# Where the low parts of the weight tiles are subtracted in a decoder trunk with product-key experts

## Chip, cores, metric

The kernel runs on one core of one Trainium2 chip. The metric is device time in microseconds (us) of one execution; less is better. The engines are called PE (TensorE), DVE (VectorE), ACT (ScalarE), POOL (GpSimd) and SP (SyncE, which only issues DMAs here).

## What is computed

Two layers over 512 tokens of width 1024: a gated linear recurrence, then latent attention. Each is followed by a PEER layer, an expert layer whose 16384 experts are single neurons that are found by product keys. The change lies in the PEER layer alone, which runs once per layer:

```python
def peer(h, w_q, sub_keys, u_tab, v_tab):
    q = (h @ w_q).reshape(B, S, 8, 2, 128)                      # 8 heads, two halves
    s = jnp.einsum('bshpd,hpnd->bshpn', q, sub_keys)            # scores against 2 x 128 keys
    v1, i1 = lax.top_k(s[..., 0, :], 16)
    v2, i2 = lax.top_k(s[..., 1, :], 16)
    cand = (v1[..., :, None] + v2[..., None, :]).reshape(B, S, 8, 256)
    cv, ci = lax.top_k(cand, 16)
    idx = e1 * 128 + e2        # e1, e2: the keys of the 16 best pairs
    g = softmax(cv)
    act = gelu(h . u_tab[idx])
    out = sum(g * act * v_tab[idx])
```

## The kernel before

**Experts without a gather.** For the first 384 of the 512 tokens (`ND`) the kernel does not gather expert rows. It computes all 16384 expert activations as dense products, 128 tiles of 128 experts (`u_part`, tensor uT), multiplies them with a gate matrix that is zero where an expert was not chosen, and multiplies the result with all 128 tiles of v. For the last 128 tokens (`gather_steps`) POOL gathers rows of u and v by indirect DMAs, 256 per layer through four row buffers (`grow`, `GROWS`), and DVE takes the dot products and the weighted sums.

**hi and lo.** float32 products are made of three passes over pairs: each operand is split into a high part, rounded by ACT (`whi`), and a low part, the difference (`wlo`). `mm3` runs lo x hi, hi x lo and hi x hi. `wtile` loads a weight tile of 128x1024 (512 KB, SP's queue, four buffers `raw`), and `split` writes the two parts into three buffers each:

```python
last = nc.scalar.activation(hi, src, AF.Copy)
lo = (eng or nc.vector).tensor_tensor(lo, src, hi.bitcast(F32), op=OP.subtract)
```

The engine of the subtraction is an argument. In the profile it is line L165, whichever engine runs it; the rounding is L164, the matmuls are L201 to L203.

**The stages of `peer`.**

1. *Scoring.* Four groups of two heads. Each group has four tiles of w_pq (three of the first group's are made ahead of it), 16 key score matmuls (`sc`), then on DVE for each block of 128 tokens the search of the 16 best (`topk_half`: maxima, their indices, their replacement, twice) and the sums of pairs (`candidates`). Behind each group come a few modulation columns (`adas`, L153, on DVE; six per group in layer 0, two in layer 1) and `UPQ[grp]` expert tiles. The last group's search for the gathered token block is decoded there too (`decode`, one-hot products `oh`), which gives POOL its indices.
2. `UDEC` = 13 more expert tiles, while DVE decodes the first block of 128 tokens.
3. *Gate stretch.* 24 groups of 16 tokens (`gate_group`): DVE makes one-hot tiles `oo` and products `pr`, PE multiplies them into the gate matrix (`wps`), ACT copies it out and writes 1 MB per group to DRAM. Between groups the loop spreads the expert tiles that are left up to `LEAD - UEND` = 86, and 74 of the gather steps (`EARLY`). An expert tile planned for group i stands on PE behind the matmuls of group i-2. From tile 27 on an expert tile's activations go to DRAM (`gsp`, 192 KB, ACT's queue).
4. Seven more expert tiles, then the products with v, with the remaining expert tiles in between.

**What sets the order.** The program is traced in the order of the source; a planner then orders each engine's queue by a timeline of its own, by priority and readiness. `issue_after` adds an order between two instructions of one engine. The numbers in `UPQ`, `UDEC` and `UEND` are written by hand.

Of the kernel before, what the change touches and what calls it, by code (L numbers as in the profile page):

```python
# [23 lines left out]
KC = D // P  # L24
# [18 lines left out]
SPILL = 66  # L43
OWN = KC * T // ND
LEAD = OWN + RING - 3 + SPILL
UPQ = (5, 6, 6, 6)
UDEC = 13
UEND = 7
QUIET = 4
# [34 lines left out]
class Trunk:  # L84
# [953 lines left out]
    def peer(self, l):  # L1038
        nc, io, tc = self.nc, self.io, self.tc
        nd = NB - 1  # L1040
        with ExitStack() as st:
# [6 lines left out]
            h = []  # L1048
# [12 lines left out]
            with own:  # L1061
                for i, hs in enumerate(HALVES):
                    for k in range(KC):
# [5 lines left out]
                        hi, lo = (p[:, hs] for p in h[k])  # L1069
# [33 lines left out]
            def ring(t):  # L1103
                held = (t - OWN) % RING < RING - 3
                return acts.tile([P, ND], F32, name="gact" if held else "gsp", bufs=RING - 3 if held else 3)

            nc.scalar.dma_start(self.xscr, self.x)

            def u_part(after=None):
                t = state["u"]  # L1110
                state["u"] = t + 1
                out = self.bank("u", True)
                hi, lo = self.wtile(io["uT"][l][t], KC, eng=nc.vector)
                with tc.issue_after(after) if after is not None else ExitStack():
                    for k, (bh, bl) in enumerate(h):
                        self.mm3(out[:, :ND], (hi[:, k, :], lo[:, k, :]), (bh[:, :ND], bl[:, :ND]), k == 0, k == KC - 1)
                if t < OWN:
                    gact[t] = self.x.rearrange("p k t -> p (k t)")[:, t * ND:t * ND + ND]
                elif LEAD - SPILL <= t < LEAD:
                    g = acts.tile([P, ND], F32, name="gsp", bufs=3)  # L1120
                    nc.scalar.activation(g, out[:, :ND], AF.Gelu)
                    nc.scalar.dma_start(self.gscr[l, t - (LEAD - SPILL)], g)
                    return
                else:
                    gact[t] = ring(t)
                nc.scalar.activation(gact[t], out[:, :ND], AF.Gelu)  # L1126
# [13 lines left out]
            def decodes(bs):  # L1140
                for b in bs:
                    res = []
                    for _ in self.decode(dpool, cvs[b], cis[b], iu[b], res):
                        yield
                    if b == nd:
                        gsel.append(self.gather_index(gpool, l, *res))
                    else:
                        prep[b] = self.gate_prep(pool, *res)

            with tc.tile_pool(name=f"pq{l}", bufs=1) as pool:  # L1150
                for grp in range(4):
                    keys = pool.tile([P, 4, P], F32, name="keys", bufs=2)
                    nc.scalar.dma_start(keys, io["keysT"][l][:, 4 * grp:4 * grp + 4, :])
                    outs = []
                    wq = l * 16 + 4 * grp
                    if grp == 0:
                        outs = pq0
                    qs = []
                    for m in range(4):
                        if m >= len(outs):  # L1160
                            outs.append(self.bank("pq"))
                            self.lin(outs[m], self.wtile(io["w_pq"][wq + m], KC, eng=nc.vector), h)
                        q = pool.tile([P, T], F32, name="pq_s", bufs=5)
                        nc.scalar.activation(q, outs[m], AF.Copy)
                        qs.append(q)
                    for b in (nd, *range(nd)):
                        sc = self.bank("sc")
                        for m in range(4):
                            nc.tensor.matmul(sc[:, m * P:m * P + P], qs[m][:, b * P:b * P + P], keys[:, m, :],
                                             start=True, stop=True)  # L1170
                        for m in range(4):
                            last = self.topk_half(pool, sc[:, m * P:m * P + P], vs[b][:, 4 * grp + m, :],
                                                  iu[b][:, 4 * grp + m, :])
                        self.candidates(pool, vs[b], cvs[b], cis[b], 2 * grp, 2)
                        if grp == 3 and b == nd:
                            for _ in decodes((nd,)):
                                pass
                            gsteps = self.gather_steps(gpool, l, *gsel[0], hn)
                    self.hold = ()
                    with tc.issue_after(last):  # L1180
                        self.adas(6 if l == 0 else 2, pool)
                    for _ in range(UPQ[grp]):
                        u_part()
            with tc.tile_pool(name=f"gate{l}", bufs=1) as pool:
                nsg = P // TG
                steps = decodes(range(nd))
                for i in range(UDEC):
                    u_part()
                while 0 not in prep:
                    next(steps)  # L1190
                n0, nt = state["u"], nd * nsg
                ds = 0
                wlast, plast = [None, None], []
                for i in range(nt):
                    more = 1 if i >= nsg and i % nsg < nsg // 2 else 0
                    while state["u"] < n0 + (LEAD - UEND - n0) * (i + 1) // nt + more:
                        u_part(after=wlast[-2])
                    w, p = self.gate_group(pool, l, i // nsg, i % nsg, *prep[i // nsg])
                    wlast.append(w)
                    plast.append(p)  # L1200
                    while ds < 7 * (i + 2) // nsg:
                        next(steps, None)
                        ds += 1
                    with tc.issue_after(plast[max(0, i - 1)]):
                        while done < min(EARLY, EARLY * (i + 1) // (nt - QUIET)):
                            next(gsteps)
                            done += 1
                while state["u"] < LEAD:
                    u_part(after=wlast[-1])
# [113 lines left out]
            outs = [hpool.tile([P, D], F32, name=f"onat{b}", tag=f"h{b}") for b in range(nd)] + [next(gsteps)]  # L1323
# [232 lines left out]
```

## Time and profile before

| | |
|---|---|
| runs shown | 2972.43, 2970.81, 2964.76 us (median 2970.81) |
| the profiled execution | 2963.21 us, span 2961.4 us |
| granted PE clock, mean | 0.990 |
| busy: PE, DVE, ACT, POOL | 2874.9, 2559.4, 1387.6, 960.9 us |
| scoring to first gate product, layer 0 and 1 | 221 to 468 us, 1744 to 1980 us |
| gate groups, layer 0 and 1 | 468 to 728 us, 1980 to 2245 us |
| DMA over the span | 274 GB/s |

How to read it: times count from the span's start. A row of a group of instructions gives line, engine, operation, output <- input, shape, count, then busy us and mean ns, then idle us before them and what ended it. A row of a window gives, for each engine, busy us and in brackets the instructions. Matmuls are pipelined, so a mean length of a matmul is more than its share of PE's time.

### The profile page before, as it was taken

The page shows a single profiled execution, that of the slowest core. Times are in us where ns is not written, and L with a number is a line of the kernel's source. Part 1 is how long each engine was busy: PE and PEld are TensorE (multiplying, and loading weights), DVE is VectorE, ACT ScalarE, POOL GpSimd, SP SyncE. Part 2 cuts the span into 40 slices and gives each one's busy share as a digit, 9 for nine tenths or more (in the row PEclk, how much of TensorE's full clock was granted, in tenths as well). Part 3 has the DMA queues.
Part 4 walks back from the last instruction along what each step waited for, and adds up shares of the span by engine and source line. Part 5 has one row for each costly group of instructions (what it writes and reads, how often), then busy time and mean ns, then how long its engine had stood idle before and what let it go on. Part 6 is the DMA issues. An engine that isn't in the chain of part 4 may idle for free.

```text
span 2961.4 us, 43899 instructions
## 1 busy us (share of the span) xinstructions
PE 2874.9 (97%) x15680; PEld 2566.0 (87%) x15680; DVE 2559.4 (86%) x4887; ACT 1387.6 (47%) x2039; POOL 960.9 (32%) x718
## 2 busy tenths in 40 slices
PE   7999999989999999999999999999999999999998
PEld 5689898989888889998778799999989888899997
DVE  8989999999888878889878888999997777888888
ACT  4753245656343333333576742456655333333333
POOL 4000003645142234535434400015643111244542
PEclk9999999999999999999999999999999999999999
DMA  8544558999999999999323334369999999999996
GB/s 317 188 139 147 173 178 305 357 371 367 307 393 359 365 321 354 319 350 324 121 83 114 120 132 136 125 216 353 362 355 370 319 335 322 310 328 354 345 333 224
DMA packets 296219, 813.71 MB, mean 275 GB/s; under 512 B 33152, under 2 KB 130560, under 8 KB 289600
## 3 DMA queue, kind: packets, MB, share of 16 engines
q1 hardware_dynamic: 188928, 439.41, 43.4%
q0 software_dynamic: 78912, 287.34, 26.9%
q10 hardware_dynamic: 28160, 84.14, 7.3%
q8 instruction: 124, 2.03, 0.3%
q14 instruction: 95, 0.78, 0.1%
HBM read 727.44 MB, written 83.36 MB: 274 GB/s over the span
## 4 chain that ended last, share of the span: by engine, by line
PE 72%; DVE 15%; issue 5%; DMA 4%; POOL 2%; ACT 2%; ACTq 0%; DVEq 0%; SPq 0%; POOLq 0%
PE acc L202 11%; PE acc L203 11%; PE acc L201 11%; PE u L201 8%; PE u L202 8%; PE u L203 8%; DVE wlo L165 3%; POOL grow L1451 2%; DVE oo L1022 1%; DMA grow<-in_u_dram,idx 1%; DVE pr L1024 1%; PE pq L202 1%; PE pq L203 1%; DMA ada_raw<-in_adaw_dram 1%; PE pq L201 1%
## 5 line engine op out<-in xcount | busy, mean ns | idle before, releaser
L1451 POOL DMA_INDIRECT grow<-in_u_dram,idx x256 | 374.8, 1464 | 1099.2 <-DVE gdot L1455 404.4
L201 PE MATMUL u<-h,wlo 128*128 128x384 f32 x2048 | 692.8, 338 | 2.0 <-DVE wlo L165 1.0
L203 PE MATMUL u<-h,whi 128*128 128x384 f32 x2048 | 688.5, 336 | 0.0
L202 PE MATMUL u<-h,whi 128*128 128x384 f32 x2048 | 687.6, 336 | 0.0
L203 PE MATMUL acc<-vh,ah 128*128 128x512 f32 x1512 | 589.4, 390 | 0.0
L202 PE MATMUL acc<-vl,ah 128*128 128x512 f32 x1512 | 589.1, 390 | 0.0
L1451 POOL DMA_INDIRECT grow<-in_v_dram,idx x256 | 411.6, 1608 | 514.5 <-DVE gacc L1460 336.5
L201 PE MATMUL acc<-vh,al 128*128 128x512 f32 x1512 | 555.8, 389 | 0.0
L165 DVE TENSOR_TENSOR wlo<-raw,whi 128x1024 fp32r<-128x1024 f32 (+1 forms) x313 | 383.3, 1226 | 85.0 <-ACT whi L164 84.9
L165 DVE TENSOR_TENSOR vl<-vraw,vh 128x1024 fp32r<-128x1024 f32 x252 | 308.4, 1224 | 125.8 <-ACT vh L164 120.5
L164 ACT ACTIVATE whi<-raw 128x1024 fp32r<-128x1024 f32 (+2 forms) x362 | 352.4, 975 | 114.9 <-issue 33.2
L201 PEld LDWEIGHTS u<-h,wlo 128*128 128x128 f32 x2048 | 386.6, 189 | 6.1 <-ACT gact L1126 1.7
L202 PEld LDWEIGHTS u<-h,whi 128*128 128x128 f32 x2048 | 386.3, 189 | 2.7
L203 PEld LDWEIGHTS u<-h,whi 128*128 128x128 f32 x2048 | 385.8, 188 | 0.1
L203 PEld LDWEIGHTS acc<-vh,ah 128*128 128x128 f32 x1512 | 283.8, 188 | 59.2
L202 PEld LDWEIGHTS acc<-vl,ah 128*128 128x128 f32 x1512 | 283.8, 188 | 57.4
L201 PEld LDWEIGHTS acc<-vh,al 128*128 128x128 f32 x1512 | 283.8, 188 | 57.0
L1460 DVE SCALAR_TENSOR_TENSOR gacc<-grow,gdot,gacc 128x1024 f32<-128x1024 f32 x254 | 325.2, 1280 | 8.9 <-DMA grow<-in_v_dram,idx 7.8
L1455 DVE CUSTOM_DVE_ANT_0 grow<-grow,hn 128x1024 f32<-128x1024 f32 x256 | 309.7, 1220 | 20.9 <-DMA grow<-in_u_dram,idx 20.6
L164 ACT ACTIVATE vh<-vraw 128x1024 fp32r<-128x1024 f32 x252 | 264.6, 1050 | 97.0 <-issue 73.5
L164 ACT ACTIVATE ah<-gact 128x384 fp32r<-128x384 f32 x204 | 106.6, 523 | 390.0 <-PE acc L203 248.5
L1033 ACT ACTIVATE stg<-wps 128x512 f32<-128x512 f32 x192 | 185.0, 1120 | 40.4 <-PE wps L193 40.4
(417 smaller groups left out, 4342.9 us busy)
## 6 DMA issues: line engine op xcount, KB each, us to landing
raw<-in_uT_dram SPq DMA_DIRECT2D x256, 512.0 KB
vraw<-in_v_dram SPq DMA_DIRECT2D x256, 512.0 KB
wscr<-stg ACTq DMA_DIRECT2D x48, 1024.0 KB
wt<-wscr SPq DMA_DIRECT2D x42, 1024.0 KB
ada_raw<-in_adaw_dram SPq DMA_DIRECT2D x76, 512.0 KB
gscr<-gsp ACTq DMA_DIRECT2D x132, 192.0 KB
gact<-gscr SPq DMA_DIRECT2D x108, 192.0 KB
ada_raw<-in_adaw_dram POOLq DMA_DIRECT2D x36, 512.0 KB
```

The source lines that it names most:

```text
L164: last = nc.scalar.activation(hi, src, AF.Copy)
L165: lo = (eng or nc.vector).tensor_tensor(lo, src, hi.bitcast(F32), op=OP.subtract)
L201: nc.tensor.matmul(out, al, bh, start=first, stop=False, **kw)
L202: nc.tensor.matmul(out, ah, bl, start=False, stop=False, **kw)
L203: last = nc.tensor.matmul(out, ah, bh, start=False, stop=last, **kw)
L1022: nc.vector.tensor_tensor(oo.rearrange(by_pair, d=2), io, toks(et), op=OP.is_equal)
L1024: prod = nc.vector.tensor_tensor(pr.rearrange(by_pair, d=2), hot, toks(gp), op=OP.mult)
L1033: nc.scalar.activation(stg[:, :, c:c + 4].rearrange("p e t -> p t e"), wps.rearrange("p (t e) -> p t e", t=4), AF.Copy, scale=1.0 / GSCALE)
L1451: nc.gpsimd.indirect_dma_start(out=row, out_offset=None, in_=tabs[s], in_offset=bass.IndirectOffsetOnAxis(ap=idx[:, k:k + 1], axis=0))
L1455: nc.vector.tensor_tensor_reduce(row, row, hn, op0=OP.mult, op1=OP.add, scale=1.0, scalar=0.0, accum_out=col)
L1460: nc.vector.scalar_tensor_tensor(acc, row, col, acc, op0=OP.mult, op1=OP.add)
```

## The change

The subtractions of the weight tiles of w_pq (all but the three that are made ahead of the first group), of the expert tiles in the scoring and of the 13 `UDEC` tiles are issued on POOL in place of DVE. `UPQ` goes from 23 to 14 tiles per layer; since the gate loop takes what is left up to tile 86, nine more tiles come to stand there, and their subtractions stay on DVE.

```diff
-UPQ = (5, 6, 6, 6)
+UPQ = (3, 3, 4, 4)
...
-            def u_part(after=None):
+            def u_part(after=None, eng=None):
...
-                hi, lo = self.wtile(io["uT"][l][t], KC, eng=nc.vector)
+                hi, lo = self.wtile(io["uT"][l][t], KC, eng=eng or nc.vector)
...
-                            self.lin(outs[m], self.wtile(io["w_pq"][wq + m], KC, eng=nc.vector), h)
+                            self.lin(outs[m], self.wtile(io["w_pq"][wq + m], KC, eng=nc.gpsimd), h)
...
                     for _ in range(UPQ[grp]):
-                        u_part()
+                        u_part(eng=nc.gpsimd)
...
                 for i in range(UDEC):
-                    u_part()
+                    u_part(eng=nc.gpsimd)
```

## Prediction

> **What bounds the kernel now.** I read the page first: its busy line and the shares of the chain that ended last.
>
> ```profile
> PE 2874.9 (97%) x15680; PEld 2566.0 (87%) x15680; DVE 2559.4 (86%) x4887; ACT 1387.6 (47%) x2039; POOL 960.9 (32%) x718
> PE 72%; DVE 15%; issue 5%; DMA 4%; POOL 2%; ACT 2%; ACTq 0%; DVEq 0%; SPq 0%; POOLq 0%
> ```
>
> TensorE (PE) is all but full, VectorE (DVE) comes next, GpSimd (POOL) idles for two thirds. So time can only come from PE's gaps, and I looked for them in the stretches that the change touches: first key scores to first gate product, and the gate groups, in both layers (windows, columns as the header says).
>
> ```profile
> core 0: us, PE busy (x) PEld busy (x) DVE busy (x) ACT busy (x) POOL busy (x), PEclk, DMA share, GB/s
> 221.00:468.00 247.00, 244.17 (x1352) 230.96 (x1352) 236.41 (x1003) 96.13 (x128) 5.40 (x4) 1.00 0.54 176
> 468.00:728.00 260.00, 242.44 (x1846) 235.73 (x1845) 254.59 (x301) 161.65 (x199) 146.80 (x69) 0.98 0.97 355
> 1744.00:1980.00 236.00, 236.00 (x1315) 224.57 (x1314) 215.10 (x970) 94.43 (x124) 5.29 (x4) 1.00 0.44 143
> 1980.00:2245.00 265.00, 249.73 (x1884) 243.92 (x1883) 254.98 (x300) 163.43 (x203) 147.75 (x69) 0.97 0.96 352
> ```
>
> While keys are scored PE is full (244 of 247 us, 236 of 236); POOL does almost nothing. In the gate stretch PE lacks 17.6 and 15.3 us, DVE is 98% and 96% busy, and DMA is at 0.97. The waits (us in total, times, longest) say for whom PE waits:
>
> ```profile
> PE wps L1030 <- DVE pr L1024: 34.2, 19, 5.6
> ```
>
> That is the gate's one-hot products: the gate stretch is bound by DVE. With PE's granted clock at 0.98 and 0.97 there (260 x 0.02 + 265 x 0.03 = 13 us), all that this change can reach is 3 + 17.6 + 15.3 + 13 = about 49 us in both layers.
>
> **The change part by part.** Per layer, `UPQ` falls from 23 to 14 tiles. Of the subtractions in `wtile`, 13 for w_pq, 14 for uT in the scoring and 13 for uT in `UDEC` go to POOL: 40. The 9 moved tiles stay on DVE, inside the gate loop.
>
> ```profile
> L165 DVE TENSOR_TENSOR wlo<-raw,whi 128x1024 fp32r<-128x1024 f32 x50 | 60.7, 1214 | 0.0
> L165 POOL TENSOR_TENSOR wlo<-raw,whi 128x1024 fp32r<-128x1024 f32 x3 | 7.2, 2386 | 22.6 <-ACT whi L164 22.6
> 1925.00:1950.00 25.00, 25.00 (x146) 25.00 (x145) 24.86 (x93) 11.87 (x16) 0.00 (x0) 1.00 0.49 151
> ```
>
> One subtraction is 1.21 us on DVE and 2.39 us on POOL. In 1925 to 1950 PE runs u matmuls alone: 25 / 146 = 0.171 us each, 24 to a tile, 4.11 us a tile. POOL's 2.39 us is under that, and three hi/lo buffers stand between, so I cost POOL's length itself at nothing; if PE ran out of prepared tiles it would cost up to 2.4 - 1.2 = 1.2 us for each.
>
> *Before the gate.* PE gets 9 x 4.11 = 37 us less work there. DVE gets about 50 subtractions less (the row above): -61 us. What DVE may lose again is the question. No row shows POOL subtracting beside the key search, but the attention stage has POOL subtractions beside DVE work (timeline: start, length, engine, line, operation):
>
> ```profile
> 1444.78 4.86 POOL L165 TENSOR_TENSOR xlo<-raw,xhi 128x1024 fp32r<-128x1024 f32 x2 [2.98 <-ACT xhi L164]
> 1446.04 0.69 DVE L340 TENSOR_TENSOR xn<-x,rs 128x512 f32<-128x512 f32 x1 [1.21 <-PE rs L325]
> 1447.93 2.25 DVE L359 TENSOR_TENSOR hml<-hf,hmh 128x512 fp32r<-128x512 f32 x1
> 1450.70 0.68 DVE L165 TENSOR_TENSOR hml<-hf,hmh 128x512 fp32r<-128x512 f32 x1
> 1467.50 2.40 POOL L165 TENSOR_TENSOR wlo<-raw,whi 128x1024 fp32r<-128x1024 f32 x1 [17.87 <-ACT whi L164]
> 1467.87 2.45 DVE L165 TENSOR_TENSOR wlo<-raw,whi 128x384 fp32r<-128x384 f32 x1 [0.37 <-ACT whi L164]
> L165 DVE TENSOR_TENSOR al<-gact,ah 128x384 fp32r<-128x384 f32 x98 | 54.5, 557 | 16.3 <-ACT ah L164 16.3
> ```
>
> The same DVE operation on hml takes 0.68 us alone and 2.25 us beside POOL, ending 0.5 us after it; a 128x384 subtraction takes 2.45 instead of 0.56, again to POOL's end. Both read two SBUF tensors. xn at 1446.04, whose rs lies in PSUM, keeps its 0.69 us in the middle of a POOL subtraction. So a two-input SBUF operation of DVE stands still until POOL has finished. The Trainium skill, SBUF — State Buffer, section "SBUF: two separate sides", says the same: one port pair, an exclusive lock for the whole instruction, against a DVE instruction with two SBUF inputs or in a 2-port mode; the trace agrees with 2.25 against 0.68 us. By "a POOL subtraction is off the path" alone the change would gain as in the first rival; by the lock it is what follows.
>
> In 221 to 468 the search itself (maximum, index, replace) has one data tensor or its scores in PSUM, so I let it pass. These have two:
>
> ```profile
> L153 DVE CUSTOM_DVE_ANT_0 ada_junk<-ada_raw,csil,vecs 128x1024 bf16<-128x1024 f32 x24 | 30.8, 1282 | 9.0 <-DMA ada_raw<-in_adaw_dram 9.0
> L929 DVE TENSOR_TENSOR cand<-v 128x128 f32<-128x128 f32 x16 | 4.4, 274 | 0.0
> L932 DVE TENSOR_TENSOR cand<-v 128x96 f32<-128x96 f32 x16 | 3.9, 241 | 0.0
> L978 DVE TENSOR_TENSOR oh<-iota_m,rc 128x1024 bf16<-128x1024 bf16 x9 | 6.2, 692 | 0.2
> 221.03 0.52 DVE L918 MAX8 v<-sc 128x8 f32<-128x128 f32 x2 [0.74 <-PE sc L1169]
> 417.25 0.29 DVE L922 FIND_INDEX8 iu<-v,s 128x8 uint32<-128x128 f32 x1
> ```
>
> The last two rows are the first and the last of the search: 196 us, less up to 37. Scoring: 27 POOL subtractions are 64 us of some 165, so an isolated two-input operation meets one with chance 0.39 and waits half of 2.39. Layer 0 has 24 ada and 16 cand pairs: 40 x 0.39 x 1.2 = 19 us; layer 1 has 8 ada: 24 x 0.39 x 1.2 = 11 us. Decode: nine rounds of oh, each with a chain of two-input operations behind it, run while the 13 `UDEC` tiles are made; nearly each of the 13 POOL subtractions meets one soon after its start, 1.5 us each, 20 us. Estimate: DVE loses 39 us in layer 0 and 31 in layer 1. Bounds: nothing, and 40 x 2.39 = 96 us, if each meets one at its start. The rows above, 1.6 and 1.9 us lost, are nearer to the upper end for one meeting; the thin traffic of two-input operations in the search pulls down the average (0.9 us per subtraction). The upper bound would put layer 0 at -61 + 96 + 17 = +52; I leave it outside the range, since it asks that each of 40 be met in its first moment. The lock holds POOL as well; its 2.39 us leave 1.7 us of each tile's 4.11 for that.
>
> When does the first gate product start?
>
> ```profile
> 468.32 2.36 DVE L1024 TENSOR_TENSOR pr<-oo,gp 128x2048 f16<-128x2048 f16 x2
> 1979.96 2.35 DVE L1024 TENSOR_TENSOR pr<-oo,gp 128x2048 f16<-128x2048 f16 x2
> L165 DVE TENSOR_TENSOR wlo<-raw,whi 128x1024 fp32r<-128x1024 f32 x19 | 23.2, 1223 | 0.9 <-ACT whi L164 0.9
> ```
>
> Layer 0: DVE was busy 236 of 247 us, so DVE sets it: -61 + 39 = -22 us. Layer 1: DVE had 21 us idle, PE paces the scores. Seven of the nine tiles lay ahead of the last key group (2 + 3 + 2): -29 us; from its search (1890.6) to 1974 DVE made the 19 subtractions of the third row, -23 us, and meets the 20 us of lock of the decode: -3. Together -32; the 11 us of the scoring lie in DVE's idle time. PE's own bound is -37 in both.
>
> *The gate stretch.* It takes on 9 tiles, 8.8 of them by the last product: DVE +8.8 x 1.22 = 11 us, to 254.6 + 11 = 265; PE +8.8 x 4.11 = 36. PE's present need is its tiles and gate matmuls at undisturbed pace: 46 u tiles (1104 matmuls by the row below) x 4.11 = 189, and 742 others at 0.056 (469.60, 469.65, 469.71) = 42, together 231.
>
> ```profile
> 468.00:728.00 260.00, 200.62 (x1104) 0.98 0.97 355
> 469.60 0.22 PE L1030 MATMUL wps<-pr,oo 128*128 128x128 f16 x1 [2.14 <-DVE pr L1024]
> 469.65 0.22 PE L193 MATMUL wps<-pr,oo 128*128 128x128 f16 x1
> 469.71 0.22 PE L1030 MATMUL wps<-pr,oo 128*128 128x128 f16 x1
> ```
>
> So PE needs 267 and DVE 265, against 260 now. Two engines at the same load wait for each other in turn; I add 10 us (now 17 of gaps with 29 us of slack on PE): 277, +17 us per layer. The floor of this term is +7. What moves along: 9 loads of 512 KB on SP's queue and 9 spills of 192 KB on ACT's, 6.3 MB. 260 us x 355 GB/s = 92.3 MB; 98.6 MB in 277 us is 356 GB/s, the rate of now, so I add nothing; were DMA the bound there, the 6.3 MB would cost 18 us, just the term taken. ACT gets 9 x (1.0 + 0.5) = 13 us on 162 of 260: hidden.
>
> Sum: layer 0 -22 + 17 = -5, layer 1 -32 + 17 = -15: **-20 us**. The profiled execution took 2963.2 us (span 2961.4), so 2943; the three runs shown have a median of 2970.8, 7.6 us above. I put forecast and rivals on the middle, 2967: 2947.
>
> *POOL's queue.* The subtractions enter it ahead of the gathers:
>
> ```profile
> 446.88 1.62 POOL L1451 DMA_INDIRECT grow<-in_u_dram,idx  x1 [0.30 <-issue]
> 472.30 1.68 POOL L1451 DMA_INDIRECT grow<-in_u_dram,idx  x1 [23.79 <-DVE gdot L1455]
> ```
>
> The fifth gather waits 23.8 us for a row buffer. A subtraction queued behind it would wait as long, and PE behind that. In program order all 40 come first; the planner may reorder. Gathers that wait for a subtraction lose 2.4 us of that 23.8: nothing.
>
> **The rivals.**
>
> *The lock hardly bites* (DVE loses under 15 us per layer). For it: most of the search has one input. Then PE sets the start: -37 + 17 = -20 each, -40: 2927.
>
> *No change.* In the decode each of the 13 POOL subtractions holds DVE for its whole length, 31 us instead of 20: layer 0 -5 + 11 = +6, layer 1 -15 + 11 = -4, together +2: 2969. For it: DVE hardly idles there, and POOL would subtract 2.39 of each 4.11 us.
>
> *The search is held too* (the other side). Replace, index and maximum of the second eight read their scores from SBUF; if they count as the two-input ones do, a subtraction in the scoring costs DVE half its length nearly always, 1.2 us, beside the 31 us of the decode: 27 x 1.2 + 31 = 63 us. Layer 0: -61 + 63 + 17 = +19. Layer 1: 32 of the scoring less DVE's 21 of idle, -29 + 11 - 23 + 31 + 17 = +7. Together +26: 2993. The sum turns where DVE loses 50 us per layer in place of 39 and 31. Against it: xn, with one input from SBUF and one from PSUM, was not held.
>
> *POOL's queue blocks*: a subtraction behind the fifth gather, some 20 us of PE per layer, -20 + 40 = +20: 2987. Against it: the order above.
>
> **How the numbers follow.** What a measurement here can tell from no change is about 0.3%, 9 us. The forecast (-35 to -9 us) has 0.45, the weak lock 0.2, no change 0.15, the held search 0.13, the blocked queue 0.07. So faster 0.65, same 0.15, slower 0.2. The forecast's own range is 2932 to 2958. The range from 2915 (the weak lock, and half the 10 us of gate waiting saved) to 2980 leaves out most of the two slow cases.
>
> **What would show it.** POOL has 80 subtractions of 128x1024 more, near 2.4 us; DVE 80 fewer. If the lock holds, ada_junk, cand and oh have means well above 1282, 274 and 692 ns in the scoring, while the search's instructions keep theirs; means as before speak for the first rival. The first pr stands near 446 and 1948 us, the gate stretch lasts some 277 us with DVE and PE both near full. I am wrong if the gate stretch keeps its 260 us, if the first pr comes no earlier, or if PE shows waits for wlo on POOL.

## The result, and the profile after

The changed kernel is slower: 3009.66 us (median, 3008.01 to 3013.23) against 2970.68 (2964.76 to 2972.43) before, ratio 1.0142 [1.0126, 1.0158], so 39 us. Its profiled execution has a span of 3006.5 us, against 2961.4.

The windows of the same stages in the changed kernel (layer 0, then layer 1; first key search to first gate product, gate groups, and from the last gate product to the first product with v):

```profile
core 0: us, PE busy (x) PEld busy (x) DVE busy (x) ACT busy (x) POOL busy (x), PEclk, DMA share, GB/s
224.00:465.10 241.10, 210.73 (x1093) 197.18 (x1093) 227.72 (x967) 81.95 (x107) 94.78 (x41) 0.94 0.44 148
465.10:736.80 271.70, 264.71 (x2002) 258.18 (x2001) 255.60 (x290) 169.05 (x209) 123.49 (x65) 0.99 0.96 352
736.80:796.60 59.80, 53.41 (x304) 52.43 (x305) 41.51 (x66) 23.63 (x34) 6.17 (x5) 0.97 0.84 272
1772.80:1990.80 218.00, 202.40 (x1079) 189.61 (x1078) 207.91 (x939) 81.55 (x106) 92.61 (x41) 0.97 0.37 121
1990.80:2279.50 288.70, 279.09 (x2072) 271.93 (x2071) 262.01 (x291) 173.18 (x217) 109.64 (x67) 0.99 0.95 342
2279.50:2322.70 43.20, 40.15 (x252) 39.35 (x251) 21.74 (x30) 17.76 (x24) 9.42 (x7) 1.00 1.04 352
```

Before, TensorE was full while keys were scored. Now it lacks 30 us there in layer 0 (241.1 - 210.7) and 16 in layer 1, at a granted clock of 0.94 and 0.97 in place of 1.00. A part of that comes with the nine moved tiles: with the move alone, run below, it lacks 18 and 2 us. The first gate product comes at 465.1 us (468.3 before), the first product with v at 796.6 (759.7 before). Counted by their matmuls, 24 to a tile, the three windows of layer 0 hold 29.2, 51.8 and 12.0 expert tiles, where they held 39.5, 46.0 and 7.0 before. So more is left for the third window, 59.8 us long where it was 31.3 in the kernel before:

```profile
728.40:759.70 31.30, 31.13 (x200) 30.96 (x201) 23.07 (x35) 14.64 (x20) 1.68 (x1) 1.00 0.95 311
```

Three readings tell what happened. First, the holds. Rows of groups in layer 0's scoring and decode, first of the changed kernel, then two of the kernel before (line, engine, operation, tile, shape, count, busy us, mean ns):

```profile
L153 DVE CUSTOM_DVE_ANT_0 ada_junk<-ada_raw,csil,vecs 128x1024 bf16<-128x1024 f32 x24 | 38.6, 1608 | 11.0 <-DMA ada_raw<-in_adaw_dram 11.0
L922 DVE FIND_INDEX8 iu<-v,s 128x8 uint32<-128x128 f32 x64 | 17.9, 280 | 0.0
...
L929 DVE TENSOR_TENSOR cand<-v 128x128 f32<-128x128 f32 x16 | 12.7, 791 | 0.0
...
L964 DVE CAST rc<-row 128x128 bf16<-128x128 f32 x3 | 5.1, 1690 | 0.0
...
L165 POOL TENSOR_TENSOR wlo<-raw,whi 128x1024 fp32r<-128x1024 f32 x37 | 91.9, 2490 | 129.6 <-ACT whi L164 129.6
```

```profile
L922 DVE FIND_INDEX8 iu<-v,s 128x8 uint32<-128x128 f32 x64 | 18.4, 287 | 0.0
...
L964 DVE CAST rc<-row 128x128 bf16<-128x128 f32 x3 | 0.7, 222 | 0.0
```

`cand` went from 274 to 791 ns, `ada_junk` from 1282 to 1608, the search's own instructions stayed. Below, "holds" is the sum, from first search to first gate product, of what VectorE operations took above the median of the same operation and shape in the kernel before, where that is over 0.15 us: 40.8 us in layer 0, 39.9 in layer 1.

Second, ScalarE's queue (timeline of the changed kernel; start, length, last the idle time before and what ended it):

```profile
354.56 1.06 ACT L164 ACTIVATE whi<-raw 128x1024 fp32r<-128x1024 f32 x1
370.34 1.06 ACT L981 ACTIVATE ib<-i4f 128x1024 bf16<-128x1024 bf16 x1 [14.73 <-DVE i4f L947]
371.31 0.47 ACT L1126 ACTIVATE gact<-u 128x384 f32<-128x384 f32 x1
371.68 1.05 ACT L164 ACTIVATE whi<-raw 128x1024 fp32r<-128x1024 f32 x1
```

`ib` is a broadcast copy of key indices that ScalarE makes for each decode step on VectorE. It stands in the queue ahead of `gact` (which empties a PSUM bank that TensorE wants) and of `whi`, the next tile's rounding. While VectorE is late, all three are late. The waits (us in total, times, longest), two rows of the changed kernel and one of the kernel before:

```profile
ACT ib L981 <- DVE oh L982: 87.3, 24, 9.2
...
PE u L201 <- ACT gact L1126: 27.7, 7, 9.5
```

```profile
ACT ib L981 <- DVE oh L982: 28.7, 13, 6.2
```

Third, the clock behind a stall (windows of 10 us of the changed kernel, TensorE alone):

```profile
350.00:360.00 10.00, 10.00 (x59) 0.99 0.87 310
360.00:370.00 10.00, 2.46 (x15) 0.86 0.76 265
370.00:380.00 10.00, 8.08 (x32) 0.62 0.15 52
```

After 7.5 us without work in the second window, 32 matmuls take 8.08 us, 0.25 each in place of 0.17. So a stall costs its length and then part of the next 10 us. The Trainium skill, TensorE: Matmul & The Clock Gate, section "Part 1: The HAM clock gate", states that the clock halves after about 3.4 us of idling and comes back after as much work. The trace agrees on the half (0.62 is the mean of this row); both times are longer here: the trace grants half the clock from 367.3 us, 4.8 us after the stall began, to 377.5, 5.6 us after it ended.

### The profile page after: what moved, and what is told of

It reads as the page before. It is cut to its first block, busy times and chain, and to the rows that moved or that the text cites. A ratio compares the mean times of both kernels' runs of the same rounds, so it can differ in the third digit from the quotient of the medians.

```text
span 3006.5 us, 43943 instructions
## 1 busy us (share of the span) xinstructions
PE 2887.4 (96%) x15680; PEld 2576.2 (86%) x15680; DVE 2563.7 (85%) x4807; ACT 1388.8 (46%) x2039; POOL 1072.3 (36%) x798
## 4 chain that ended last, share of the span: by engine, by line
PE 78%; DVE 14%; issue 3%; DMA 2%; ACT 2%; POOL 1%; SPq 0%; ACTq 0%; DVEq 0%; POOLq 0%
PE acc L202 12%; PE acc L203 12%; PE acc L201 12%; PE u L201 10%; PE u L202 9%; PE u L203 9%; DVE ada_junk L153 1%; PE wps L1030 1%; PE pq L202 1%; PE pq L203 1%; PE pq L201 1%; PE wps L193 1%; DMA ada_raw<-in_adaw_dram 1%; DVE wlo L165 1%; DVE iu L922 1%
## 5 line engine op out<-in xcount | busy, mean ns | idle before, releaser
L201 PE MATMUL u<-h,wlo 128*128 128x384 f32 x2048 | 701.4, 342 | 52.9 <-ACT gact L1126 27.7
L203 PE MATMUL u<-h,whi 128*128 128x384 f32 x2048 | 696.5, 340 | 0.0
L202 PE MATMUL u<-h,whi 128*128 128x384 f32 x2048 | 695.8, 340 | 0.0
L1451 POOL DMA_INDIRECT grow<-in_u_dram,idx x256 | 343.9, 1343 | 671.3 <-DVE gdot L1455 454.6
L1451 POOL DMA_INDIRECT grow<-in_v_dram,idx x256 | 359.0, 1402 | 581.4 <-DVE gacc L1460 399.2
L164 ACT ACTIVATE whi<-raw 128x1024 fp32r<-128x1024 f32 (+2 forms) x362 | 352.9, 976 | 213.0 <-PE u L203 92.8
L202 PEld LDWEIGHTS u<-h,whi 128*128 128x128 f32 x2048 | 391.9, 191 | 2.6
L203 PEld LDWEIGHTS u<-h,whi 128*128 128x128 f32 x2048 | 391.4, 191 | 0.0
L165 POOL TENSOR_TENSOR wlo<-raw,whi 128x1024 fp32r<-128x1024 f32 (+2 forms) x129 | 244.9, 1904 | 351.2 <-ACT whi L164 347.6
L165 DVE TENSOR_TENSOR wlo<-raw,whi 128x1024 fp32r<-128x1024 f32 x233 | 286.2, 1229 | 73.4 <-ACT whi L164 70.2
L1455 DVE CUSTOM_DVE_ANT_0 grow<-grow,hn 128x1024 f32<-128x1024 f32 x256 | 309.4, 1219 | 16.4 <-DMA grow<-in_u_dram,idx 16.2
L164 ACT ACTIVATE ah<-gact 128x384 fp32r<-128x384 f32 x204 | 106.8, 524 | 418.8 <-PE acc L203 317.1
L164 ACT ACTIVATE vh<-vraw 128x1024 fp32r<-128x1024 f32 x252 | 264.3, 1049 | 68.4 <-issue 50.1
```

The source lines that it names most:

```text
L201: nc.tensor.matmul(out, al, bh, start=first, stop=False, **kw)
L202: nc.tensor.matmul(out, ah, bl, start=False, stop=False, **kw)
L203: last = nc.tensor.matmul(out, ah, bh, start=False, stop=last, **kw)
L1451: nc.gpsimd.indirect_dma_start(out=row, out_offset=None, in_=tabs[s], in_offset=bass.IndirectOffsetOnAxis(ap=idx[:, k:k + 1], axis=0))
L1455: nc.vector.tensor_tensor_reduce(row, row, hn, op0=OP.mult, op1=OP.add, scale=1.0, scalar=0.0, accum_out=col)
```

## The experiments

All ratios are against the kernel before, which was run again beside each group of runs (medians 2966.4 to 2970.7 us). "First gate product" and "first product with v" are times from the start of the span, layer 0 and 1.

| kernel | us | ratio | holds | first gate product | first product with v |
|---|---|---|---|---|---|
| before | 2970.7 | | 0, 0 | 468.3, 1980.0 | 759.7, 2277.6 |
| changed | 3009.7 | 1.0142 [1.0126, 1.0158] | 40.8, 39.9 | 465.1, 1990.8 | 796.6, 2322.7 |
| move only | 2962.2 | 0.9971 [0.9959, 0.9984] | 18.9*, 0 | 451.8, 1959.9 | 773.1, 2277.1 |
| GpSimd only | 3016.1 | 1.0163 [1.0131, 1.0195] | 53.3, 47.1 | 481.9, 2028.8 | 773.7, 2330.0 |
| GpSimd in the scoring only | 2971.0 | 0.9999 [0.9987, 1.0011] | 16.8, 16.2 | 454.5, 1960.9 | 772.1, 2278.8 |
| GpSimd in the decode only | 3001.4 | 1.0121 [1.0104, 1.0138] | 20.7, 24.6 | 454.2, 1972.0 | 767.2, 2309.7 |
| no copy on ScalarE | 3000.7 | 1.0101 [1.0074, 1.0129] | 40.2, 36.7 | 464.1, 1989.1 | 784.8, 2314.4 |
| two buffers for the copy | 3003.8 | 1.0122 [1.0105, 1.0139] | 40.8, 40.7 | 464.5, 1987.1 | 782.6, 2319.4 |
| four pieces | 2991.7 | 1.0088 [1.0071, 1.0104] | 25.2, 22.6 | 448.4, 1974.3 | 781.4, 2304.7 |
| roundings first | 2982.0 | 1.0044 [1.0029, 1.0060] | 41.4, 38.5 | 465.5, 1980.6 | 778.3, 2297.9 |
| roundings first, four pieces | 2954.5 | 0.9953 [0.9937, 0.9969] | 19.8, 17.8 | 448.5, 1948.6 | 764.8, 2264.4 |
| unread repeat on GpSimd | 3048.3 | 1.0277 [1.0260, 1.0295] | 25.9, 26.0 | 469.2, 2033.5 | 813.8, 2350.6 |
| move only, two buffers for the copy | 2961.3 | 0.9972 [0.9961, 0.9983] | 0, 0 | 448.3, 1958.7 | 764.5, 2276.0 |
| five tiles moved, no GpSimd | 2962.2 | 0.9974 [0.9965, 0.9983] | 0, 0 | 461.2, 1971.0 | 767.6, 2278.5 |

The text below takes differences of medians. By the ratios some come out otherwise: 12 us in place of 9 for the run without the copy, 16 in place of 18 for the four pieces, 29 in place of 28 for the roundings first.

*Some 108 instructions of this one profile, most of them of the search, are some 0.17 us longer, with GpSimd idle; what it was stays open, and it is not seen in layer 1 nor in the same kernel with two copy buffers.

**Which part of the change?** First the move of nine tiles alone, with every subtraction on VectorE.

```diff
-UPQ = (5, 6, 6, 6)
+UPQ = (3, 3, 4, 4)
```

> The nine tiles move (UPQ 3, 3, 4, 4), every subtraction stays on DVE. Theory A (POOL's subtractions hold DVE, DVE's delay holds ACT's queue, and PE starves behind it): without POOL there is no such hold; DVE has the same work in another place, so 0 to +10 us against before (2971 to 2981), DVE's two-input operations at their old lengths. Theory B (the move alone did it: too little PE work while keys are scored, too much behind): nearly the whole loss, +30 to +45 us (3000 to 3016).

2962.2 us, better than either theory had it: the move does no harm, it gains 0.3%. It brings the first gate product 16.5 us forward in layer 0.

Then GpSimd alone, with the old numbers of tiles.

```diff
-UPQ = (3, 3, 4, 4)
+UPQ = (5, 6, 6, 6)
```

> The 49 subtractions ahead of the gate go to POOL, UPQ stays at 5, 6, 6, 6. Theory A: DVE still loses some 40 us per layer to POOL and ACT still waits for DVE with the roundings behind it; the loss stays, +10 to +35 us against before. Theory B: the loss goes, -20 to 0 us against before.

3016.1 us, 46 us above the kernel before, where the first theory had at most 35: the whole loss is GpSimd's. Next, the changed kernel with the 13 decode tiles back on VectorE.

```diff
                 for i in range(UDEC):
-                    u_part(eng=nc.gpsimd)
+                    u_part()
```

> As the changed kernel, but the 13 tiles ahead of the gate are subtracted on DVE again; POOL has the 27 of the scoring. Theory A: the hold falls from 40 to some 20 us per layer, DVE gets 16 us of subtractions back, so DVE is as late as before, but the tiles no longer need POOL behind ACT: 5 to 20 us better than the changed kernel (2990 to 3005). Theory B: as the changed kernel, within 5 us (3005 to 3015).

2971.0 us, better than either theory had it. The 27 subtractions of the scoring cost some 9 us against the move alone, though they hold VectorE for 16 us a layer. The 39 us hang on 13 subtractions a layer. The complement, GpSimd in the decode alone, was run later:

```diff
-                            self.lin(outs[m], self.wtile(io["w_pq"][wq + m], KC, eng=nc.gpsimd), h)
+                            self.lin(outs[m], self.wtile(io["w_pq"][wq + m], KC, eng=nc.vector), h)
...
-                        u_part(eng=nc.gpsimd)
+                        u_part()
```

> The changed kernel with the subtractions of the scoring stretch (weights of the queries and the expert tiles after each group of keys) on VectorE again, so that GpSimd has only the 13 tiles of the decode. If these 13 are the whole cause by themselves, the time is the one of the move alone plus the 39 us that lay between the changed kernel and the one with the decode on VectorE: 2995 to 3005. If they cost so much only because the scoring has put VectorE behind by then (an interaction), it is 2965 to 2980.

3001.4 us: the 13 do it by themselves, without a backlog from the scoring. In this run the loss fell on layer 1; in layer 0 the first product with v is even 6 us ahead of the move alone.

**Through what? ScalarE's copy taken away.** VectorE multiplies with the broadcast indices directly.

```diff
-                ib = pool.tile(shp, BF, name="ib", bufs=1)
-                nc.scalar.activation(ib, i4f[...].to_broadcast(shp), AF.Copy)
-                nc.vector.tensor_tensor(oh, oh, ib, op=OP.mult)
+                nc.vector.tensor_tensor(oh, oh, i4f[...].to_broadcast(shp), op=OP.mult)
```

> As the changed kernel, but the decode's product reads the index tile spread over 16 columns directly; ACT's copy ib, which waited 58 and 45 us for DVE in front of the roundings, is gone, and DVE pays some 0.4 us more for each of 16 products per layer. Theory A: the waits of PE for u tiles ahead of the gate (some 35 and 20 us) mostly go: 20 to 40 us better than the changed kernel (2970 to 2990). Theory B, and a theory C (POOL's own 2.4 us per tile is what PE waits for): within 8 us of the changed kernel.

3000.7 us, 9 us better only, so neither theory's number. The edit carried a price of its own. The multiply, with the copy and without it (the first row from the move alone, the second from this run):

```profile
L982 DVE TENSOR_TENSOR oh<-oh,ib 128x1024 bf16<-128x1024 bf16 x9 | 6.3, 698 | 0.4
L980 DVE TENSOR_TENSOR oh<-oh,i4f 128x1024 bf16<-128x1024 bf16 x10 | 14.2, 1422 | 0.1
```

Ten of them are 7 us more for VectorE (2 of these are one hold: one took 3.27 us, the others 1.17 to 1.23). And ScalarE's exponential of the gates took the copy's place in the queue (timeline of this run):

```profile
373.61 0.31 ACT L950 ACTIVATE g<-g 128x128 f32<-128x128 f32 x1 [14.91 <-DVE g L949]
```

14.91 us of waiting where the copy had waited 14.73. So this run did not take the suspected chain away. A gentler edit gives the copy a second buffer.

```diff
-                ib = pool.tile(shp, BF, name="ib", bufs=1)
+                ib = pool.tile(shp, BF, name="ib", bufs=2)
```

> The changed kernel with two buffers in place of one for ib, the copy that ScalarE makes for each decode step, so that ScalarE no longer stands in its queue until VectorE has multiplied with the copy before (87 us of such waits in the changed kernel, 29 before). The roundings behind it in the queue can go out one step sooner. Theory A (ScalarE's queue, held up by a late VectorE, is what starves TensorE): the waits fall to under 30 us, TensorE's waits for wlo before the first gate group (18.7 and 9.0 us) mostly go, and the time falls by 10 to 25 us, to 2985 to 3000. If ScalarE's wait only mirrors VectorE's own lateness (theory L or W), it is 3003 to 3012.

3003.8 us, a miss: the waits of the copies on VectorE stayed at 81.7 us (87.3). The trace says why: the first two copies now go out one behind the other (368.6 and 369.5 us), and each later one stands one step earlier in the queue, in the places where the copies stood before, and again starts only behind a multiply (387.3 us behind the one of 386.5, and so on). The roundings stay behind them, so this run did not take the chain away either.

**Through what? Shorter holds.**

```diff
-        lo = (eng or nc.vector).tensor_tensor(lo, src, hi.bitcast(F32), op=OP.subtract)
+        full, n = lo, lo.shape[1] // parts          # parts: 4 for what the change put on GpSimd, else 1
+        for j in range(parts):
+            c = slice(j * n, j * n + n)
+            lo = (eng or nc.vector).tensor_tensor(full[:, c], src[:, c], hi[:, c].bitcast(F32), op=OP.subtract)
```

> The changed kernel, with each GpSimd subtraction of a weight tile done as four pieces of 128x256 in place of one of 128x1024. If a VectorE operation is held until the GpSimd instruction beside it ends (theory L), a hold is now at most about 0.6 us instead of 2.4, the excess of VectorE operations before the first gate group (40.8 us in the first layer, 39.9 in the second) falls to about 10, and the time to about 2970 to 2980. If the loss is the longer way of a tile through GpSimd (theory W: a subtraction of 2.4 us that starts late makes TensorE wait, whoever is held), the way is as long or a little longer, and the time stays at 3005 to 3020 whatever the excess does.

2991.7 us, 18 us less, between the two theories, and holds of 25 and 23 us, not the 10 expected: a piece still catches an operation, and there are four times as many. Two groups of layer 0:

```profile
L168 POOL TENSOR_TENSOR wlo<-raw,whi 128x256 fp32r<-128x256 f32 x146 | 116.6, 829 | 88.2 <-ACT whi L164 88.2
...
L932 DVE TENSOR_TENSOR cand<-v 128x128 f32<-128x128 f32 x16 | 6.7, 422 | 0.0
```

GpSimd works longer for a tile (4 x 829 = 3316 ns, 2490 in one piece) and the kernel is faster all the same. So it is not the length of the way through GpSimd that costs, and the holds are at least a part of the loss. Whether they are all of it this run can't tell: it took away 16 of some 40 us of holds a layer, and 18 of the 39 us.

The rival test was a miss of its own making: all subtractions on VectorE, and GpSimd repeats the 13 of the decode into a tile that nobody reads.

```diff
             self.split(hi[:, :kc, :m], lo[:, :kc, :m], r, eng or nc.gpsimd)
+            if shadow:
+                dum = shadow.tile([P, KC, P], BF, name="dum", bufs=1)
+                nc.gpsimd.tensor_tensor(dum, r, hi[:, :kc, :m].bitcast(F32), op=OP.subtract)
```

> The kernel with the move alone (2962 us: nine tiles moved, all subtractions on VectorE), and beside each of the 13 tiles that run with the decode GpSimd computes the same difference a second time into a tile of bf16 that nobody reads. No consumer waits for GpSimd, but it runs at the same place with the same operands. Theory L (VectorE held): the holds of the changed kernel come back, 20 to 25 us a layer, and as VectorE does its own 13 subtractions too (16 us a layer) the time is 2990 to 3015. Theory W (late subtractions on GpSimd): nobody waits for them, and the time stays at 2960 to 2967.

3048.3 us. The holds came out as expected (25.9 and 26.0 us), but a second stall hides what they cost. GpSimd's first repeat:

```profile
408.87 4.99 POOL L185 TENSOR_TENSOR dum<-raw,whi 128x1024 bf16<-128x1024 f32 x2 [222.71 <-DVE mod L153]
```

It starts only after the scoring (the last search ended at 394.1 us), while the tiles that it reads wait with their buffers taken, and TensorE stood still for 47 us until 417.5. The unread tile lies in the pool that opens after the scoring's; that its memory came free so late is my reading and was not tried. The run says nothing on the rivals.

**The order of ScalarE's queue.** What is left is the chain of the second reading. Between the first copies of the first decode in layer 1, ScalarE's roundings (rows restricted to line L164; instructions in brackets) in the kernel before, then the changed one:

```profile
1900.00:1917.60 17.60, 5.27 (x5) 1.00 0.37 120
1918.00:1931.30 13.30, 3.16 (x3) 1.00 0.36 119
1932.00:1943.50 11.50, 3.17 (x3) 1.00 0.54 172
```

```profile
1900.60:1917.80 17.20, 3.17 (x3) 1.00 0.37 119
1918.40:1932.20 13.80, 3.16 (x3) 0.88 0.35 106
1932.80:1945.10 12.30, 2.11 (x2) 1.00 0.29 87
```

The copies are as far apart as before: VectorE lost its subtractions and got holds in their place. But its queue mates changed. 5, 3 and 3 roundings stood between the copies, now 3, 3 and 2, and a rounding is a tile, 4.11 us of TensorE: three tiles are 12 us of work for some 18. The order is laid down when the program is built; that the planner counted on a VectorE without these subtractions and without holds is an inference, the order itself is seen. So the four copies of the first decode in each layer were put later in the queue; nothing else in the source was changed:

```diff
+                for ib, t in zip(self.ibs, (14, 18, 22, 25)):     # the first decode's copies
+                    tc.add_manual_dep(ib, his[t].name, ...)       # behind the rounding of tile t
```

> The changed kernel with four entries of ScalarE's queue put later: the four copies ib of the first decode stand behind the roundings of the 15th, 19th, 23rd and 26th expert tile of the layer. In the changed kernel's queue 3, 3 and 2 roundings stand between these copies, though VectorE needs 18, 14 and 13 us from one copy to the next and TensorE 4.1 us a tile; here 4, 4 and 3, as in the kernel with the move alone. Theory Q (the order of ScalarE's queue was laid out for a VectorE without the 1.2 us subtractions, and the holds make it as slow as with them, so TensorE runs out of tiles between two copies): the waits of TensorE for u<-wlo before the first gate group (18.7 and 9.0 us) fall below 8 a layer, the slower clock behind them goes too, and the time falls by 15 to 25 us, to 2985 to 2995, with the holds of VectorE unchanged at about 40 us a layer. Theory L alone (VectorE's holds lengthen the decode, and that is what TensorE waits for whatever the order): 3003 to 3012.

2982.0 us, 28 less than the changed kernel and a little better than expected, with the holds as they were. (For the move alone the expectation has 4, 4 and 3; its trace shows 5, 3 and 3, as before.) The same intervals of layer 1:

```profile
1892.20:1913.80 21.60, 4.11 (x4) 1.00 0.34 105
1914.40:1928.70 14.30, 4.05 (x4) 0.88 0.36 116
1929.40:1941.80 12.40, 3.16 (x3) 1.00 0.40 126
```

and TensorE in them, the changed kernel ahead of this one:

```profile
1918.40:1932.20 13.80, 12.80 (x65) 0.88 0.35 106
1932.80:1945.10 12.30, 9.45 (x54) 1.00 0.29 87
```

```profile
1914.40:1928.70 14.30, 14.30 (x75) 0.88 0.36 116
1929.40:1941.80 12.40, 12.40 (x74) 1.00 0.40 126
```

In the first interval TensorE lacks 2.1 us, about as before (1.8 in the changed kernel); in the other two nothing is missing any more, though the clock in the second is 0.88 as it was. The copies' waits for VectorE's multiply fell from 87.3 to 10.0 us. In layer 0 one part of the expectation missed: TensorE's waits for tiles did not fall below 8 us there (25, of which 12.4 are one wait that ends at 377.0 us and that the profile puts down to `gact`, as it does the 18.7 and 9.0 us of the changed kernel that the expectation calls waits for wlo), though the first product with v came 18 us sooner. Where the gain lies is seen in layer 0, in the first and the third window of this run:

```profile
220.20:465.50 245.30, 214.46 (x1134) 201.13 (x1133) 227.98 (x960) 83.54 (x108) 95.53 (x41) 0.94 0.44 150
...
743.50:778.30 34.80, 34.65 (x222) 34.17 (x221) 31.34 (x52) 18.90 (x25) 0.00 (x0) 1.00 0.85 283
```

The first gate product comes no sooner (465.5 us, 465.1 in the changed kernel), but TensorE has 30.9 expert tiles behind it by then in place of 29.2, and 7.8 are left for the third window in place of 12.0. In layer 1 it is 30.9 in place of 28.6, and the gate stretch lasts 275.9 us in place of 288.7. What the edit names is four entries of one queue. The exponentials of the first decode kept their places among the roundings, but further on the planner moved copies of the next decode and some operations of VectorE as well, so a part of the 28 us may be theirs.

Order and pieces together:

> The order of the run before (copies of the first decode put behind 4, 4 and 3 roundings) and the GpSimd subtractions in four pieces of 128x256. The pieces alone took 18 us off the changed kernel (2991.7) and left 23 to 25 us of holds a layer in place of 40. If holds and queue order are two parts of one loss that add, this run is 2970 to 2980; if the pieces had already removed what the order costs, it is 2988 to 2994.

2954.5 us, better than either theory had it and better than the sum: the two together take 55 us off the changed kernel, by themselves 28 and 18. It is 0.47% faster than the kernel before and the lowest median here, though its interval overlaps those of the kernels without GpSimd. Here the first gate product does come sooner, at 448.5 and 1948.6 us:

```profile
224.00:448.50 224.50, 209.40 (x1134) 197.08 (x1133) 207.12 (x959) 83.44 (x108) 123.97 (x150) 0.97 0.49 163
```

**Two tries at a faster kernel without GpSimd.** Move alone and two copy buffers:

> The kernel with the move alone (all subtractions on VectorE, nine tiles moved to the gate stretch) and two buffers for ib. A try for a faster version: ScalarE waits 13 us a layer for that one buffer there, but TensorE waits little (18.5 and 1.9 us before the first gate group), so 2955 to 2965, against 2962 with one buffer.

2961.3 us, 0.9972 [0.9961, 0.9983]: as with one buffer. Five tiles moved in place of nine (23 to 18; the expectation says four), `UPQ = (4, 4, 5, 5)`:

> The kernel before with four tiles moved in place of nine (4, 4, 5 and 5 after the four groups of keys), all subtractions on VectorE. Nine moved tiles gave 2962, none 2970. If what the move brings is the earlier end of the decode (first gate group 16 and 20 us sooner) less the longer gate stretch, half of it gives 2963 to 2969; if there is a best point between, 2955 to 2962.

2962.2 us, 0.9974 [0.9965, 0.9983]: as with nine.

## Why the prediction was wrong, by its steps

*The step that failed* is the one that sets what is done ahead of the gate: "DVE was busy 236 of 247 us, so DVE sets it: -61 + 39 = -22 us", and -32 in layer 1. The stretch from first search to first gate product shrank by 6 us in layer 0 (247.3 to 241.1) and by 18 in layer 1 (235.8 to 218.0). I added up each engine's work and let the largest sum set the end. Two things were wrong in that.

The larger one is a term that was not there. ScalarE has one sentence in the prediction, for the gate stretch ("13 us on 162 of 260: hidden"), and none ahead of the gate. The question who stands behind a waiting instruction was asked for GpSimd's queue and not for ScalarE's. There the decode's copies wait for VectorE, with TensorE's tiles behind them. The missing term is 28 us by the run with the roundings put first. It does not show in the stretch to the first gate product, which is no shorter in that run in layer 0 and about as long in layer 1 (245.3 and 217.0 us, 241.1 and 218.0 in the changed kernel), but in the tiles that TensorE has done by then: those that are missing are done after it, in layer 0 in the third window, which the prediction did not have, in layer 1 in the gate stretch.

The other is the size of VectorE's sum. In layer 0 its busy time fell from 236.7 to 227.7 us, by 9 and not by 22, though the holds came as costed. The subtractions freed 49 us and not 61. Four of them were still made there, and a row's time counts twice what overlaps with the next instruction: in the kernel before, all other work of VectorE covers 183.0 of the 236.7 us, which leaves 53.7 for the subtractions, not the 61.9 of their row, and in the changed kernel they have 4.3. So layer 0 is -49 + 40 of longer work + 3 of idle time = -6 us. By the same count layer 1 is -49 + 42 - 11 = -18 us, where -32 was put together from three parts; which of these failed stays open.

Of the 63 us between the forecast and the measured time, 28 go with the order of the queue, 27 more came back when the pieces were added to it, and 8 are left. That the fastest kernel's 2954.5 us lies in the forecast's own range (2932 to 2958), and its first gate products (448.5 and 1948.6 us) near the 446 and 1948 foreseen, doesn't confirm the sum: its holds are halved. With the queue in order and the holds whole, as costed, the time is 2982.0, 35 us above the forecast.

*The signs.* Of the three signs of being wrong one came: the first gate product was 3 us earlier in layer 0 and 11 later in layer 1. The gate stretch grew, and no expert tile in the changed kernel waits for a subtraction on GpSimd.

*The lock* was right in kind and nearly in size: 39 and 31 us foreseen, 40.8 and 39.9 measured; 20 us foreseen for the 13 decode subtractions, 20.7 and 24.6 with these alone on GpSimd. In layer 0 the closeness is partly luck: 8.5 of the 40.8 us (6.4 in layer 1) fell on operations with one SBUF input, which were counted as free. What a hold costs was not the same everywhere: 16 us of holds in the scoring went into VectorE's slack and cost 9 us over both layers, those of the decode cost the 39. Shorter holds gave back 18.

*GpSimd's length at nothing* was nearly right. The waits of the kernel with the roundings first:

```profile
ACT ib L981 <- DVE oh L982: 10.0, 8, 4.1
...
PEld u L201 <- POOL wlo L165: 9.5, 3, 4.3
```

TensorE's weight loads for expert tiles wait 9.5 us in the whole run for a subtraction on GpSimd.

*The gate stretch* was right on average: +17 foreseen in each layer, 271.7 and 288.7 us measured (+11.6 and +22.5), and 277.7 and 277.8 in the fastest kernel, where TensorE is not disturbed ahead of it. DMA stayed at 0.95 to 0.96 of its time (0.98 in the fastest kernel), as costed.

*The rivals.* The weak lock and the held search are both refuted by the rows above (`cand` held, the index search at 280 ns). GpSimd's queue did not block: the last subtraction of layer 0 ran at 444.6 us, ahead of the fifth gather at 469.0. "No change" had the right place, the decode, but by VectorE's sum alone it gave 2969. None of them had ScalarE's queue.

## What to carry to other kernels

When work moves off an engine, look at what the other engines' in-order queues have interleaved with that engine's results: the order is fixed when the program is built, so if the engine does not get faster by as much as it lost in work, what is queued behind its results can run dry, as TensorE did here. Count, between two such waits, how much work the queue lets through and compare it with the time between them. And where two engines hold each other, look for slack: here 16 us of holds a layer in the scoring cost 9 us over both layers, 21 to 25 in the decode cost 39, and cutting the subtractions into shorter pieces gave back 18.

## What the runs showed of the hardware

Operations of VectorE with a single input from SBUF are held by GpSimd too, where I had counted on two-input ones alone (timeline of the changed kernel, with two operations of VectorE beside one pair of subtractions, and one, with two inputs, beside another):

```profile
378.50 4.77 POOL L165 TENSOR_TENSOR wlo<-raw,whi 128x1024 fp32r<-128x1024 f32 x2 [3.32 <-ACT whi L164]
378.81 2.18 DVE L959 TENSOR_SCALAR off<-row 128x128 f32<-128x128 f32 x1
380.92 2.44 DVE L964 CAST rc<-row 128x128 bf16<-128x128 f32 x1
...
435.60 4.64 POOL L165 TENSOR_TENSOR wlo<-raw,whi 128x1024 fp32r<-128x1024 f32 x2
435.13 5.21 DVE L985 TENSOR_TENSOR oh<-oh 128x128 bf16<-128x128 bf16 x1
```

`off` and `rc` take 0.22 us undisturbed. The Trainium skill, SBUF — State Buffer, section "SBUF: two separate sides", counts a VectorE instruction in a 2-port mode among those that are locked out; that these two run in such a mode no run here shows, but their holds agree with it. `off` ended with the first subtraction of its pair and `rc` with the second. The last two rows show that a hold isn't always bounded by one subtraction: an operation of 0.22 us, begun 0.5 us ahead of a pair, was kept until both had finished, 5.21 us, and TensorE's transposes of the decode's result waited behind it. Why one operation came in between two subtractions and the other did not stays open.
